# Dilated attention: the values of the class-by-class groups computed over token tiles, and brought to class order through DRAM

## The chip, the cores and the metric

The kernel runs on one core of one Trainium2 chip. The metric is the device time of one execution in microseconds (us), taken as the median over runs; lower is better. One execution with the hardware profiler on gives the trace from which the rows below are read.

The engines have short names in the rows: PE is TensorE (matrix products), PEld its loading of the stationary operand ("weights" of a product, whatever they hold), DVE is VectorE, ACT is ScalarE, POOL is GpSimd, SP is SyncE, which here issues transfers. A name with q at its end (SPq) is the queue of an engine.

## The reference, cut to what matters

The program is a network of two blocks. The first has a token mixer over 512 tokens of 1024 features; one of the mixer's two branches is dilated attention with three groups of four heads of 128 channels. Group 0 has dilation 1, group 1 dilation 4, group 2 dilation 16. A query attends to keys that are a multiple of the dilation before it, and the three groups' outputs are weighted by a softmax over their denominators:

```
proj = h @ w_in                                   # queries, keys, values of all groups, side by side
for gi, (win, dil) in enumerate(ATT_GROUPS):      # (128, 1), (512, 4), (2048, 16)
    aq, ak, av = parts[4 + 3 * gi], parts[5 + 3 * gi], parts[6 + 3 * gi]
    ...
    o, lse = dilated_group(heads(aq, ...), heads(ak, ...), heads(av, ...), tab, win, dil)
...
wts = softmax(stack(lses), axis=0)
att = einsum('gbhs,gbhsd->bshd', wts, stack(outs)).reshape(B, S, 512)
```

With 512 tokens, groups 1 and 2 attend only among tokens that are equal modulo 4. The change concerns `av` of these two groups alone: the product of the normalised input `h` (512 tokens by 1024 features) with 256 columns of `w_in` at a time.

## The kernel before, in words

`h` is kept feature-major on the chip: eight tiles `s.hh[k]` and eight `s.hl[k]` of 128 features by 512 tokens, the coarse and the fine part of each number. A panel of weights (`panel`) is loaded from DRAM in full precision (tile `wr`, two buffers, by SP) and split into a coarse part `wh` by ACT (L145) and a fine part `wl` by DVE (L134), each in two halves of four feature tiles, four buffers each, so two panels. Every product of two such numbers is three matmuls, `mm3` at L197, L198 and L199: coarse with coarse, coarse with fine, fine with coarse.

`gemm_a` gives feature-major results: the weights are the stationary operand and all 512 tokens move past them. `gemm_b` gives token-major results: 128 tokens of `h` are the stationary operand, a contiguous slice `s.hh[k][:, sl]`, and 256 columns of weights move. One token tile of 256 columns is 8 feature tiles by 3 matmuls, so 24 matmuls into one PSUM tile `mm` (three buffers).

`dilated` (L861) handles the four heads in two pairs. For each pair it first computes the values, 256 columns for each of three groups. Group 0's go through `gemm_b` into `av`. Those of groups 1 and 2 are wanted class by class: four classes of 128 tokens (token 4i + r is row i of class r). The kernel before takes them so from the product: the stationary operand is every fourth token of `h`, a view with a step of four elements:

```
classes = lambda t: t.rearrange("p (i r) -> p r i", r=4)
...
for k in range(KT):
    self.mm3(ps, classes(s.hh[k])[:, r], classes(s.hl[k])[:, r], w.hi(k), w.lo(k), k == 0, k == KT - 1)
nc.scalar.copy(v[:, r], ps)
```

That is L890; ACT copies each finished tile into `avc` (L891). A pair has 2 groups x 4 class tiles, so the program has 16 such tiles of 24 matmuls. The class values are used much later in the pair, by L978, after queries, keys, scores and the softmax: `po` is accumulated from `avc` as stationary operand and the transposed weights of the softmax `apc`. Then follow, for each of the pair's two heads, six panels of queries and keys (128 columns, 24 matmuls of 512 moving tokens each) by `gemm_a`.

Each engine runs its own instructions in a fixed order. SP's queue holds the loads of the weight panels: a load waits until its `wr` buffer has been split. The splitting of a panel's half waits until PE has read the same half of the panel two before it. POOL is used for some transfers (issued in software) and a few elementwise operations elsewhere in the program.

Of the kernel before, what the change touches and what calls it, by code (L numbers as in the profile page):

```python
# [37 lines left out]
class Stream:  # L38
    """One token stream: feature-major residual, its tokens and modulation."""
# [13 lines left out]
    def parts(self, n=2):  # L53
        """Views of the stream by tokens."""
        res = []
        for i in range(n):
            p = Stream(self.n // n, ctx=self.ctx)
            p.sl = slice(i * p.n, (i + 1) * p.n)
            p.of, p.col = self, self.col
            for nm in ("x", "hh", "hl"):  # L60
                if getattr(self, nm) is not None:
                    setattr(p, nm, [t[:, p.sl] for t in getattr(self, nm)])
            res.append(p)
        return res
# [14 lines left out]
class Net:  # L79
# [71 lines left out]
    def rsqrt(self, h, n):  # L151
        """1/sqrt(v) of a small fp32 tile, given -v/2: estimate from its bits and Newton steps."""
# [15 lines left out]
    def panel(self, src, r0, kt, c0, ncol, maps=False):  # L168
        """Columns of a weight matrix in two parts; maps: 4 heads x 2 maps x 32 columns, map by map."""
# [31 lines left out]
    def gemm_a(self, w, kt, ncol, s, evac, ks=None, ms=None):  # L201
        """Feature-major products: evac(m, stream, psum [128 features, tokens])."""
# [8 lines left out]
    def gemm_b(self, w, kt, ncol, s, evac):  # L211
        """Token-major products: evac(token tile, stream, psum [128 tokens, columns])."""
        for tt in range(s.nt):
            sl = slice(tt * P, (tt + 1) * P)
            ps = self.ps((P, ncol))
            for k in range(kt):
                self.mm3(ps, s.hh[k][:, sl], s.hl[k][:, sl], w.hi(k), w.lo(k), k == 0, k == kt - 1)
            evac(tt, s, ps)

# [1 line left out]
    def columns(self, items, tag, eng=None):  # L221
        """items: (name, DRAM rows [r, 128]); returns name -> [128, r] columns."""
# [18 lines left out]
    def squares(self, xs, acc=None, ks=range(KT), g=None):  # L241
        """Sum of squares over feature tiles (times a gain), added to acc."""
# [12 lines left out]
    def rms_cols(self, xs, n, acc=None, r=None):  # L255
        """1/rms per token (of x * r), token-major [128, n/128]."""
# [16 lines left out]
    def bcast(self, r, nt, tag="at"):  # L273
        """Token-major columns [128, nt] to every partition: [128, nt*128]."""
# [6 lines left out]
    def norm(self, s, r=None):  # L281
        """1/rms of every token, on all partitions."""
# [3 lines left out]
    def apply(self, s, acol, bcol, ks=range(KT)):  # L286
        """h = x * rstd * a + b, split in two parts."""
# [13 lines left out]
    def pair(self, s):  # L301
        """The two parts of a stream's eight feature tiles."""
# [13 lines left out]
    def ada_tasks(self, src, vec, conds):  # L316
        """Tasks for columns vec*1024.. of cond @ src + bias; conds: (silu cols, out cols, bias cols)."""
# [21 lines left out]
    def ada_first(self, src, cs, o, b):  # L339
        """The first two vectors, by halves of the features: one on TensorE, one on DVE."""  # L340
# [30 lines left out]
    def ada_finish(self, acc, o, b, vec, halves=(0, 1), when=lambda ins: ins):  # L371
        """Sum over partitions of the accumulated products, plus the bias."""
# [10 lines left out]
    def scale1(self, g, sc):  # L383
        """g * (1 + sc)"""
# [5 lines left out]
    def feed_forward(self, w1, w2, streams, between=None, first=None, last=None, late=None):  # L390
        """x += g2 * relu(h @ w1)^2 @ w2 for streams that share the weights, by groups of the hidden width.

        first: two parts for the first panels, and what to do before the last products of the former;
        last: (part of a stream, what to do after its products) for the last panel; late: what to do before it."""
# [52 lines left out]
    def project_norm(self, w_src, pairs, acols, bcols, ks=None):  # L447
        """x += g1 * (y @ w), then the modulated norm of x; what feed_forward is to do first.

        The streams (two, or two halves of one) take turns, so that one's norm hides behind the other's products."""  # L450
# [34 lines left out]
    # ==== first block ====================================================  # L485
    def first_block(self):
# [17 lines left out]
        # x to feature-major, with its mean squares on the way  # L504
# [74 lines left out]
        # gate of the retention branch  # L579
# [17 lines left out]
        # gate of the attention branch, attention output, merge  # L597
# [48 lines left out]
    def first_norm(self, xs, g):  # L646
        """The norm that closes the first block, then the input of the second."""
# [29 lines left out]
    def bias_tables(self):  # L677
        """Relative-position bias by distance as Toeplitz tables in DRAM."""
# [19 lines left out]
    def retention(self, s, w_in, v):  # L698
# [45 lines left out]
        def scores(dec, q, k):  # L744
            """Decayed scores, keys on partitions."""
# [34 lines left out]
        def outputs(hd, sc, v, between):  # L780
            """Token-major outputs, normalised over the head's channels, then feature-major."""
# [79 lines left out]
    def dilated(self, s, w_in):  # L861
        """Dilated attention, its three groups under one softmax.

        The first group keeps the tokens' order. The others attend only among tokens that are equal modulo 4,
        so theirs is class by class: 4 classes of 128 tokens, each a block of its own."""
# [11 lines left out]
        for pair in range(2):  # L877
            vv = []
            for g in range(3):
                w = self.panel(w_in, 0, KT, 6144 + g * 1536 + 1024 + pair * 256, 256)  # L880
                if g == 0:
# [3 lines left out]
                    continue  # L885
                v = self.t([P, 4, 256], "avc")
                for r in range(4):
                    ps = self.ps((P, 256))
                    for k in range(KT):
                        self.mm3(ps, classes(s.hh[k])[:, r], classes(s.hl[k])[:, r], w.hi(k), w.lo(k), k == 0, k == KT - 1)  # L890
                    nc.scalar.copy(v[:, r], ps)  # L891
                vv.append(v)
            for hp in range(2):
# [64 lines left out]
                # the first group's weights, keys on partitions: queries of block 1's keys, then of blocks 0, 2, 3  # L958
# [27 lines left out]
    def weigh(self, perm, both):  # L986
        """Factors of two softmax parts under a common one, each in its own order of the tokens.

        both[:, 0]: [128, part, 4, (maximum, sum)], the first part's tokens in order, the second's class by class.
        Each part's figures go to the other's order by a product that spreads them, between masks that pick."""  # L990
# [29 lines left out]
    # ==== second block ===================================================  # L1020
# [24 lines left out]
    def second_loads(self):  # L1045
        """Constants of the second block and the context, on their way to the chip."""
# [27 lines left out]
    def second_setup(self, ld):  # L1074
        """What the loads allow: context feature-major, bias rows, constants of the first layer."""
# [7 lines left out]
        # neighbourhood bias rows widened to 64 offsets, replicated for Toeplitz reads  # L1083
# [36 lines left out]
    def layer_consts(self, l, c):  # L1120
        nc = self.nc
        # spatial gating: weights transposed, norm vectors on every partition
# [5 lines left out]
        # differential attention: lambda and the scaled norm gain  # L1128
# [14 lines left out]
    def nbias(self, l, h):  # L1143
        """Negated neighbourhood bias of a head, [128 queries, 3 kinds of column window, 8 rows, 32 columns].

        Queries of a block are 8 rows by 16 columns, so the offsets between them and the keys step evenly
        through the replicated table."""
# [13 lines left out]
    def fourier(self, w_in, s, y):  # L1161
        """Real part of the transform over channels and tokens.

        Tokens k*nt + r of the output come from sums over blocks of 128 tokens of the input, weighted by powers
        of -1 and -i, with a transform of 128 tokens each; the weighted sums are formed before the channels'
        transform, the imaginary ones (classes 1 and 3 of four) after it."""
# [63 lines left out]
    def gelu2(self, out, ps):  # L1230
        """Twice the tanh-form gelu."""
# [8 lines left out]
    def gating(self, w_in, s, y, c, l):  # L1240
# [12 lines left out]
        # of twice the activation: a quarter of its variance, half of the gain  # L1253
# [24 lines left out]
    def heads(self, w, s, o, scale=None):  # L1278
        """Queries or keys of the differential branch, with their rotary embedding: o [4 heads x 32, map, part, tokens]."""
# [17 lines left out]
    def keys_values(self, w_in, s, fill=iter(()), ahead=False):  # L1297
        """Keys and values of both attention branches."""
# [32 lines left out]
    def windows(self, v, tag):  # L1331
        """Values by column window: [128 = 4 rows x 32 columns, window, half of the rows, 256]."""
# [33 lines left out]
    def attend_values(self, e, vs, head, po, eng=None):  # L1366
        """Transpose a [128 queries, keys] tile, then multiply by the values of a head and its neighbour."""
# [16 lines left out]
    def neighbour(self, yn, head, qb, qn, kx, kc, st, vx, vc, bt, po):  # L1384
        """Softmax attention of one head over the neighbourhood (if bt) and the context; logits come negated."""
# [37 lines left out]
    def stack(self, dst, src, head, sel):  # L1423
        """Both maps of a head as four stacked parts with tokens on the free axis, by TensorE."""
# [11 lines left out]
    def ctx_stacks(self, s, head, st):  # L1436
        """Stacked queries and keys of a context head."""
# [9 lines left out]
    def stacks(self, s, head, st=None):  # L1447
        """Stacked queries and keys of both branches for a head, moved between partitions by DMA."""
# [20 lines left out]
    def differential(self, s, yd, ssq, head, qb, qst, kst, vs, c, po):  # L1469
# [16 lines left out]
        # first map less lambda times the second, in units of the first one's denominator  # L1486
# [14 lines left out]
    def diff_norm(self, s, yd, ssq, h0, h1):  # L1501
        """Norm over the channels of each head."""
# [9 lines left out]
    def begin(self, s, l, step=KT):  # L1512
        """Modulated input of a layer's mixer, by steps of feature tiles; x spilled meanwhile."""
# [342 lines left out]
```

## Time and profile before

| what | value |
|---|---|
| runs before, median of 3 | 2887.05 us |
| lowest and highest | 2879.89 and 2893.06 us |
| the profiled execution, first to last instruction | 2886.3 us |
| PE busy in it | 2826.1 us (98%) |
| DVE, ACT, POOL busy | 1711.2, 1064.5, 103.5 us |
| mean granted TensorE clock | 0.992 of full speed |

The trace gives no time of the profiled execution apart from the span of its instructions; that span stands 0.75 us below the median of the runs. A busy share says only how long an engine was not idle; matmuls overlap each other in it, so PE can be busy all the time and still be slow. How fast it goes is read from the distance between the starts of matmuls or between finished tiles.

### The profile page before, as it was taken

Reading aid. Unit: us, or ns where it says so; the run is one execution under the profiler, and the core shown is the slowest. Engines: PE = TensorE matmul, PEld = TensorE weight load, DVE = VectorE, ACT = ScalarE, POOL = GpSimd, SP = SyncE. Lnnn points to the kernel's source line nnn. Section 1 sums busy time; section 2 is a strip of 40 time slices with the busy share of each in tenths; the row PEclk is TensorE's granted clock in tenths of the full one; section 3 lists DMA queues with packets and bytes.
Section 4 is the critical chain, followed back from the end, with each engine's and each line's share of the span. In section 5 each row is a group of like instructions: output and inputs, shape, how many; then the busy total and the mean of one; then the engine's idle time right before and its main releaser. Section 6 shows DMA issues by size and latency. Waiting matters only on the chain.

```text
span 2886.3 us, 38355 instructions
## 1 busy us (share of the span) xinstructions
PE 2826.1 (98%) x15364; PEld 2400.8 (83%) x15364; DVE 1711.2 (59%) x3154; ACT 1064.5 (37%) x1982; POOL 103.5 (4%) x143
## 2 busy tenths in 40 slices
PE   7999999999999999998999999999999999999999
PEld 4888888989888888778887788888888988888887
DVE  6667776252466888788648663443445848654434
ACT  4433432132334233245437442222223537433323
POOL 3000000000002000001000100000000000100000
PEclk9999999999999999999979999999999999999999
DMA  7455344131345555755324321112112433333231
GB/s 268 137 176 189 131 134 137 55 116 49 109 136 185 180 181 193 233 179 165 98 55 103 107 77 60 59 59 73 59 59 84 141 101 81 117 102 99 91 101 60
DMA packets 269124, 342.16 MB, mean 119 GB/s; under 512 B 18360, under 2 KB 218162, under 8 KB 268688
## 3 DMA queue, kind: packets, MB, share of 16 engines
q1 hardware_dynamic: 254880, 315.19, 34.8%
q10 hardware_dynamic: 10896, 14.72, 1.5%
q0 software_dynamic: 3168, 9.79, 1.2%
q8 instruction: 121, 1.98, 0.3%
q14 instruction: 59, 0.48, 0.1%
HBM read 313.38 MB, written 18.41 MB: 115 GB/s over the span
## 4 chain that ended last, share of the span: by engine, by line
PE 84%; DVE 8%; DMA 5%; ACT 2%; issue 1%; SPq 0%; DVEq 0%; POOL 0%; ACTq 0%
PE mm L198 24%; PE mm L197 24%; PE mm L199 24%; PE po L1380 2%; DVE wl L134 2%; DVE ada L141 2%; DMA wr<-in_ada_w 1%; PE tr L1374 1%; DMA wr<-in_w_in 1%; DMA wr<-in_w_ada 1%; PE s L1481 1%; ACT wh L145 1%; DMA wr<-in_w_ff 1%; PE tr L377 1%; PE at L197 1%
## 5 line engine op out<-in xcount | busy, mean ns | idle before, releaser
L134 DVE TENSOR_TENSOR wl<-wr,wh 128x1024 fp32r<-128x1024 f32 (+1 forms) x442 | 495.2, 1126 | 410.1 <-ACT wh L145 400.9
L145 ACT CAST wh<-wr 128x1024 fp32r<-128x1024 f32 (+1 forms) x442 | 425.7, 969 | 838.9 <-PE mm L198 674.0
L197 PE MATMUL mm<-h,wh 128*128 128x512 f32 (+1 forms) x1712 | 651.3, 382 | 3.6 <-ACT h L131 2.6
L198 PE MATMUL mm<-h,wh 128*128 128x512 f32 (+1 forms) x1712 | 654.1, 383 | 0.4 <-DVE h L141 0.4
L199 PE MATMUL mm<-h,wl 128*128 128x512 f32 (+1 forms) x1712 | 653.5, 383 | 0.5 <-DVE wl L134 0.5
L197 PEld LDWEIGHTS mm<-h,wh 128*128 128x128 f32 x1712 | 320.6, 188 | 67.9 <-ACT h L131 3.9
L198 PEld LDWEIGHTS mm<-h,wh 128*128 128x128 f32 x1712 | 321.3, 188 | 66.8 <-DVE ada L141 1.7
L199 PEld LDWEIGHTS mm<-h,wl 128*128 128x128 f32 x1712 | 321.6, 188 | 61.4 <-DVE wl L134 0.9
L198 PE MATMUL mm<-mid,wh 128*128 128x512 f32 (+1 forms) x864 | 335.0, 388 | 0.2 <-DVE mid L134 0.2
L197 PE MATMUL mm<-mid,wh 128*128 128x512 f32 (+1 forms) x864 | 334.7, 388 | 0.0
L199 PE MATMUL mm<-mid,wl 128*128 128x512 f32 (+1 forms) x864 | 334.1, 387 | 0.0
L141 DVE SCALAR_TENSOR_TENSOR ada<-wr,cs,ada 128x1024 f32<-128x1024 f32 x168 | 212.5, 1279 | 35.0 <-DMA wr<-in_ada_w 22.8
L197 PE MATMUL mm<-wh,h 128*128 128x256 f32 x704 | 212.1, 301 | 0.0
L199 PE MATMUL mm<-wh,h 128*128 128x256 f32 x704 | 211.1, 300 | 0.0
L198 PE MATMUL mm<-wl,h 128*128 128x256 f32 x704 | 210.9, 300 | 0.0
L131 ACT ACTIVATE f<-mm 128x256 f32<-128x256 f32 (+2 forms) x192 | 99.5, 520 | 263.0 <-PE mm L199 260.9
L198 PEld LDWEIGHTS mm<-mid,wh 128*128 128x128 f32 x864 | 162.2, 188 | 36.7 <-DVE mid L134 1.3
L199 PEld LDWEIGHTS mm<-mid,wl 128*128 128x128 f32 x864 | 162.2, 188 | 36.3
L197 PEld LDWEIGHTS mm<-mid,wh 128*128 128x128 f32 x864 | 162.2, 188 | 35.6
L141 DVE SCALAR_TENSOR_TENSOR x<-mm,modx,x 128x512 f32<-128x512 f32 (+1 forms) x116 | 84.8, 731 | 175.6 <-PE mm L199 174.1
L134 DVE TENSOR_TENSOR f<-f 128x512 f32<-128x512 f32 (+2 forms) x172 | 99.4, 585 | 143.6 <-ACT f L131 142.5
L198 PEld LDWEIGHTS mm<-wl,h 128*128 128x128 f32 x704 | 150.9, 214 | 0.8 <-issue 0.2
(451 smaller groups left out, 4309.5 us busy)
## 6 DMA issues: line engine op xcount, KB each, us to landing
wr<-in_w_ff SPq DMA_DIRECT2D x96, 1024.0 KB
wr<-in_w_in SPq DMA_DIRECT2D x69, 1024.0 KB
wr<-in_ada_w SPq DMA_DIRECT2D x48, 1024.0 KB
wr<-in_w_ada SPq DMA_DIRECT2D x16, 1024.0 KB
wr<-in_w_in SPq DMA_DIRECT2D x24, 512.0 KB
awr<-in_w_ada SPq DMA_DIRECT2D x16, 512.0 KB
wr<-in_w_ret_out SPq DMA_DIRECT2D x8, 1024.0 KB
wr<-in_w_out SPq DMA_DIRECT2D x8, 1024.0 KB
```

Of the source, the lines that this page charges most:

```text
L131: return self.nc.scalar.activation(out=out, in_=in_, func=func, **kw)
L134: return self.nc.vector.tensor_tensor(out=out, in0=a, in1=b, op=op)
L141: return self.nc.vector.scalar_tensor_tensor(out=out, in0=a, scalar=s, in1=b, op0=op0, op1=op1)
L145: self.nc.scalar.copy(hi, src)
L197: mm(out, lhsT=ah, rhs=bh, start=start, stop=False)
L198: mm(out, lhsT=ah, rhs=bl, start=False, stop=False)
L199: mm(out, lhsT=al, rhs=bh, start=False, stop=stop)
L377: when(self.nc.tensor.transpose(ps[:, j], acc[:, m * P:(m + 1) * P], self.ident))
L1374: self.nc.tensor.transpose(tp[:, i], e[:, (b0 + i) * P:(b0 + i + 1) * P], self.ident)
L1380: self.nc.tensor.matmul(po, lhsT=pt[:, kb], rhs=vs[kb][:, head // 2 * P:(head // 2 + 1) * P], start=kb == 0, stop=kb == nk - 1)
L1481: nc.tensor.matmul(ps[:, k0:k1], lhsT=qst[:, mp, qs], rhs=kst[:, mp, k0:k1], start=True, stop=True)
```

## The change

The 16 class tiles become 16 token tiles: `gemm_b` computes the values of groups 1 and 2 as it does those of group 0. ACT copies each token tile from PSUM into half of a scratch tile `f` (pool of five). After each second tile POOL issues a transfer of 256 KB from it to a DRAM tile `vcls` of 512 tokens by 256 columns. After the fourth, POOL issues one transfer of 512 KB from `vcls` to `avc`, in which partition i takes rows 4i to 4i + 3, a contiguous piece of 4 KB; so `avc` holds token 4i + r at partition i, class r, as before. L978 then reads the same `avc`. All comments and docstrings of the file are also taken out, which moves line numbers by 8 behind this place and nothing else.

```
@@ -883,12 +883,20 @@
                     vl = self.r([P, 4, 256], "av")
                     self.gemm_b(w, KT, 256, s, lambda tt, s_, ps: self.split(ps, vh[:, tt], vl[:, tt]))
                     continue
+
+                d = self.tc.dram_tile([512, 256], F32, name="vcls")
+                halves = []
+
+                def evac(tt, s_, ps):
+                    if tt % 2 == 0:
+                        halves.append(self.t([P, 2, 256], "f"))
+                    nc.scalar.copy(halves[-1][:, tt % 2], ps)
+                    if tt % 2:
+                        nc.gpsimd.dma_start(out=d[(tt - 1) * P:(tt + 1) * P].rearrange("(t p) f -> p t f", p=P),
+                                            in_=halves[-1])
+                self.gemm_b(w, KT, 256, s, evac)
                 v = self.t([P, 4, 256], "avc")
-                for r in range(4):
-                    ps = self.ps((P, 256))
-                    for k in range(KT):
-                        self.mm3(ps, classes(s.hh[k])[:, r], classes(s.hl[k])[:, r], w.hi(k), w.lo(k), k == 0, k == KT - 1)
-                    nc.scalar.copy(v[:, r], ps)
+                nc.gpsimd.dma_start(out=v, in_=d.rearrange("(i r) f -> i r f", r=4))
                 vv.append(v)
             for hp in range(2):
```

In the order of instructions, PE, DVE and SP have the same rows before and after (the matmuls keep their shapes; only which columns of `h` they load differs). On ACT, in the stretch of a pair's class values, these rows stood before (a number behind x counts equal rows in a run):

```order
L145 CAST wh<-wr 128x1024
L891 COPY avc<-mm 128x256 x3
L145 CAST wh<-wr 128x512
L891 COPY avc<-mm 128x256
L145 CAST wh<-wr 128x512
```

And these stand there now:

```order
L145 CAST wh<-wr 128x1024
L893 COPY f<-mm 128x256 x3
L145 CAST wh<-wr 128x512
L893 COPY f<-mm 128x256
L145 CAST wh<-wr 128x512
```

Only the copy's destination differs; the splitting of the next panels keeps its place behind the third and the fourth copy. On POOL, before, nothing stood between the setup of the dilated attention (`perm`, `apt`) and the loads for the second block (`xt`, `blk`):

```order
L868 DMA perm_4576<-in_k_perm 128x384
L876 MEMSET apt_4578 128x128 x3
L876 MEMSET apt_4579 128x128 x3
L1054 DMA xt_7782<-in_ctx_2 128x1024
L1054 DMA xt_7783<-in_ctx_2 128x1024
L1056 DMA blk_7786<-in_k_blk 128x2
```

Now twelve transfers stand between them, three for each of four groups of values; these are the first two groups' (the first pair's):

```order
L876 MEMSET apt_4578 128x128 x3
L876 MEMSET apt_4579 128x128 x3
L895 DMA vcls_4754<-f_4780 128x2x256
L895 DMA vcls_4754<-f_4834 128x2x256
L899 DMA avc_4863<-vcls_4754 128x1024
L895 DMA vcls_4875<-f_4901 128x2x256
L895 DMA vcls_4875<-f_4955 128x2x256
L899 DMA avc_4984<-vcls_4875 128x1024
L895 DMA vcls_5880<-f_5906 128x2x256
```

Each L899 waits until both writes of its `vcls` have landed, and the rows behind it on POOL wait with it.

## Rows read from the trace of the kernel before

**Rows 1.** The page: span, busy time of the engines, and the chain's shares by engine.
```profile
span 2886.3 us, 38355 instructions
PE 2826.1 (98%) x15364; PEld 2400.8 (83%) x15364; DVE 1711.2 (59%) x3154; ACT 1064.5 (37%) x1982; POOL 103.5 (4%) x143
PE 84%; DVE 8%; DMA 5%; ACT 2%; issue 1%; SPq 0%; DVEq 0%; POOL 0%; ACTq 0%
```

**Rows 2.** Three stretches: group 0's token tiles, then class tiles of either pair.
```profile
core 0: us, PE busy (x) PEld busy (x) DVE busy (x) ACT busy (x) POOL busy (x), PEclk, DMA share, GB/s
505.10:516.00 10.90, 10.90 (x97) 10.90 (x96) 5.45 (x9) 3.72 (x6) 0.00 (x0) 1.00 0.48 146
518.00:562.60 44.60, 44.60 (x197) 44.60 (x198) 5.73 (x14) 4.37 (x10) 0.00 (x0) 1.00 0.09 24
664.00:708.80 44.80, 44.80 (x192) 44.80 (x192) 4.45 (x6) 5.50 (x12) 0.00 (x0) 1.00 0.09 24
```

**Rows 3.** ACT in order of time, first pair: start, duration, line, operation, idle before.
```profile
508.04 0.37 ACT L145 CAST av<-mm 128x256 fp32r<-128x256 f32 x1 [1.38 <-PE mm L199]
...
516.20 0.37 ACT L145 CAST av<-mm 128x256 fp32r<-128x256 f32 x1 [0.31 <-PE mm L199]
...
523.57 0.37 ACT L891 COPY avc<-mm 128x256 f32<-128x256 f32 x1 [6.05 <-PE mm L199]
...
562.76 0.37 ACT L891 COPY avc<-mm 128x256 f32<-128x256 f32 x1 [2.18 <-PE mm L199]
...
565.28 0.62 ACT L145 CAST wh<-wr 128x512 fp32r<-128x512 f32 x1 [1.63 <-PE mm L198]
...
570.78 0.62 ACT L145 CAST wh<-wr 128x512 fp32r<-128x512 f32 x1 [1.62 <-PE mm L198]
```

**Rows 4.** ACT in order of time, first and last class copy of the second pair.
```profile
669.46 0.37 ACT L891 COPY avc<-mm 128x256 f32<-128x256 f32 x1 [4.33 <-PE mm L199]
...
709.04 0.37 ACT L891 COPY avc<-mm 128x256 f32<-128x256 f32 x1 [2.21 <-PE mm L199]
```

**Rows 5.** Weight loads of one line: token tiles (505.2 to 516), class tiles (523.6 to 562.6).
```profile
L198 PEld LDWEIGHTS mm<-wl,h 128*128 128x128 f32 x32 | 6.0, 188 | 0.0
...
L198 PEld LDWEIGHTS mm<-wl,h 128*128 128x128 f32 x56 | 18.5, 330 | 0.0
```

**Rows 6.** PE's waits, 500 to 850 us: total, times, longest (first and last of five).
```profile
PE tr L964 <- DVE apt L134: 1.2, 1, 1.2
...
PE tr L964 <- DVE sr L138: 0.2, 1, 0.2
```

**Rows 7.** SP's queue: issue of three weight panels of 512 KB (start, duration).
```profile
519.91 0.37 SPq L165 DMA_DIRECT2D wr<-in_w_in  x1
...
542.01 0.37 SPq L165 DMA_DIRECT2D wr<-in_w_in  x1
...
564.41 0.37 SPq L165 DMA_DIRECT2D wr<-in_w_in  x1
```

**Rows 8.** A panel of 1 MB on the chain of waits; the rate of transfers in one us.
```profile
638.75 5.02 DMA wr<-in_w_in
...
644.00:645.00 1.00, 1.00 (x12) 1.00 (x11) 0.81 (x7) 1.00 (x2) 0.00 (x0) 1.00 1.10 349
```

**Rows 9.** First reads of the class values, either pair: ns min/median/max, first and last start.
```profile
L978 PE MATMUL po<-apc,avc x16: 275/275/377, 616.6 to 618.4; 128*128 128x128 f32 x16
...
L978 PE MATMUL po<-apc,avc x32: 275/275/377, 762.6 to 809.7; 128*128 128x128 f32 x32
```

**Rows 10.** POOL: two kinds of its transfers (us to landing), its longest issue, two neighbours in time.
```profile
ebuf<-erow POOLq DMA_DIRECT2D x16, 240.0 KB, 7.3
xt<-in_ctx POOLq DMA_DIRECT2D x2, 512.0 KB, 3.8
...
L1107 POOL DMA_DIRECT2D acc<-in_sgu_w x2 | 1.6, 808 | 61.7 <-PE tr L262 61.7
...
858.37 0.54 POOL L1054 DMA_DIRECT2D xt<-in_ctx  x1 [438.25 <-DVE f L134]
```

## The prediction

> **What bounds the kernel now.** I read the page first. PE is busy for 98% of the span and holds 84% of the chain that ended last [rows 1]: time taken from PE's own stream comes off the end, unless PE then has to wait for something. A busy share does not say how fast PE goes, so the next view was that of busy time by stretches, over the place of the change. PE is busy all through, with the granted clock at 1.00, both where it makes group 0's token tiles and where it makes the class tiles [rows 2]. But it does 97 matmuls in 10.9 us in the first stretch and 197 in 44.6 us in the second. Same engine, same clock, same shape of matmul, half the rate.
>
> The distance between finished tiles gives the exact price, since every tile of either kind is 24 matmuls. ACT takes a token tile out of PSUM at 508.04 us and the third one after it at 516.20 [rows 3]: 8.16 / 3 = 2.72 us a tile, 113 ns a matmul. It takes the first class tile at 523.57 and the seventh after it at 562.76 [rows 3]: 39.19 / 7 = 5.599 us a tile, 233 ns a matmul. In the second pair the same seven steps run from 669.46 to 709.04 [rows 4]: 39.58 / 7 = 5.654 us.
>
> What differs between the two kinds is only the stationary operand: contiguous columns of `h` in the one, every fourth column in the other. The rows of the weight loads show it there: the same instruction takes 188 ns in token tiles and 330 ns in class tiles [rows 5]. The durations of one instruction overlap and are partly modelled, so I use them for where the time sits and not for how much; the amount is from the tile steps.
>
> Last I read PE's waits from 500 to 850 us, which hold the whole dilated attention. There are five, from 1.2 us down to 0.2 us, 2.8 us in all, and each is for DVE or ACT in the softmax; none is for a weight panel [rows 6]. So here PE sets the pace and the panels keep up.
>
> **What goes away.** 8 class tiles at 5.599 and 8 at 5.654 become 16 token tiles at 2.72 us: 8 x 2.879 + 8 x 2.934 = 23.0 + 23.5 = 46.5 us. The lower bound of a tile after is that of group 0's row, the same shapes from the same `h`; I know no reason for it to be faster. If the second pair kept its 1% more (5.654 to 5.599), its tiles would take 2.75 us and the sum would lose 0.2 us.
>
> **What is added on ACT and PE: nothing.** ACT's copies keep number, place and size, 0.37 us each [rows 3], with another destination. PE has the same 384 matmuls. A PSUM tile must be emptied in time: three buffers, a tile every 2.72 us, and between two copies at most one split of 0.62 us for a later panel [rows 3]. Group 0 lives with the same arrangement at this rate today, and PE shows no wait there.
>
> **What is added on POOL and in DRAM.** Twelve transfers: eight writes of 256 KB, four reads of 512 KB. POOL is idle around them: its next instruction before the change starts at 858.37 us after 438 us of idle time [rows 10], so neither their issues (at most 0.81 us each, the longest that POOL shows [rows 10]) nor the wait of each read for its two writes delays other work of POOL. Queued behind a waiting read are the next group's writes; they hold `f` tiles, but a pair uses four of the five, and the second pair comes some 100 us after the first.
>
> The bounce is new to this trace in this place, so I bound it from both sides. POOL's transfers land in 3.8 us (512 KB from DRAM) to 7.3 us (240 KB within DRAM) [rows 10]. The last write and the read, one behind the other, then take 2 x (0.5 + 3.8) = 8.6 to 2 x (0.8 + 7.3) = 16.2 us; I take the longer. The cover is long: the last class copy of the first pair ends at 563.13 us [rows 3] and PE's first product that needs `avc` starts at 616.6 [rows 9], 53.5 us later; in the second pair it is 709.41 [rows 4] to 762.6 [rows 9], 53.2 us. Both ends move by the same amount, so 37 us are left over. Cost: nothing. Without that cover it would be 16.2 us for each pair.
>
> **What comes closer: the weight panels.** A panel's load is issued once the `wr` tile two before it is split, and panels now follow each other faster. The loads to look at are those for the queries and keys behind the class tiles. One is issued at 519.91, before the class tiles begin to tell; the next at 542.01, after the first class group [rows 7], and ACT splits it at 565.28 [rows 3], 23.3 us later. One whole class group lies between; it shrinks from 22.4 to 10.9 us, so 11.8 us are left. The third is issued at 564.41 [rows 7] and split at 570.78 [rows 3]; both are behind the class tiles, so its 6.4 us stay. A panel of 1 MB, twice the size, landed in 5.02 us [rows 8], so both loads land in time if they have the queue alone.
>
> Now they share the transfer engines with the bounce. At the rate that the trace shows under full load, 349 GB/s [rows 8], the last write and the read of a group, 786 KB together, take 2.25 us. Behind them a panel would land in at most 5.02 + 2.25 = 7.3 us: 0.9 us over the third load's 6.4. If that falls together in both pairs it costs 1.8 us. A panel of half the size should need some 1.5 us less, and the read starts only after its writes have landed, by which time the panel mostly has too. I take 0, and keep 1.8 as the bound.
>
> **Sum.** 2886.3 - 46.5 = 2839.8 us for an execution like the profiled one. Its span is 0.75 us below the median of the runs, so the median after should be 2840.5; I say 2840.
>
> **Rivals.** First: *the gain is partly given back to late panels.* If a panel waits behind the whole landing of the read (7.3 + 0.5 us) and not just for its share of the bandwidth, it is late by 5.02 + 7.8 - 6.4 = 6.4 us, about 13 us over both pairs: 2853 us. For it: both use the same 16 transfer engines. Against: DMA is busy for 9% in the class stretches [rows 2], and the two kinds are in different queues.
>
> Second: *no change.* If the slower rate did not come from the step of four, the token tiles would run at 233 ns a matmul and the time would stay at 2886 us. Against it: in the rows nothing else differs between the two stretches [rows 2, 5]. A rule of the Trainium skill ("TensorE: Matmul & The Clock Gate", section "LDWEIGHTS (loading the stationary operand)") gives a weight load as columns / 1.2 in ns, 107 ns for 128, and makes it depend on the number of columns alone. By that rule both kinds of tile would cost the same and this edit would save nothing. The trace differs: 188 and 330 ns for the same 128 columns.
>
> Third, *slower:* the read of the bounce lands after PE wants `avc`. The place is L978, with the softmax and the output of the head queued behind it. It would begin to cost when the bounce takes more than 53 us, and eat the whole gain at 53 + 23 = 76 us for each pair, 4.7 times the longest estimate; at 90 us the time would be 2886.3 + 2 x 14 = 2914 us. What could stretch it so far is POOL being kept from issuing. The Trainium skill ("SBUF — State Buffer", section "A bandwidth-pool intuition that's wrong (but worth ruling out)") says that an issue of POOL can be blocked by DVE, 620 ns growing to 3100 ns beside a copy. Against the rival: DVE is busy for 5.7 of the 44.6 us of the class stretch [rows 2], and POOL's longest issue in the whole trace is 0.81 us [rows 10]. Even 3.1 us for each of three issues of a group stays inside the cover.
>
> **How the numbers follow.** The forecast, 2840 us, gets 0.90; late panels, 2853, 0.05; no change, 2886, 0.03; slower, 2914, 0.02. The three runs before lie from 2879.89 to 2893.06, 7 below and 6 above the median, and two medians of such runs are compared. Around 2840 I therefore take 8 us downwards, and upwards 9, which also takes in the 1.8 us of the panels, the 0.2 us of the second pair and two thirds of the way to the first rival: 2832 to 2849. What lies outside is the other rivals and some scatter, less than 2 in 10. A measurement of this kernel can tell about 0.5% (14 us) from no change. The forecast and the first rival are both beyond that, so faster 0.95, same 0.03, slower 0.02.
>
> **What would show it.** In the profile after: steps of 2.7 us between the copies into `f`; the weight loads of these tiles at 188 ns; a stretch of about 21.8 us for the two groups of a pair where there were 44.8; no wait of PE for `wl` or `wh` in the queries and keys behind it; `avc` landed some 40 us before L978, which shows no wait for a transfer. Wrong would be: steps that stay above 5 us (second rival), waits of PE for panels of more than 2 us (first), a wait of L978 for DMA (third), or a time that comes back elsewhere, in the panels of the second block, which nothing in this trace would explain.

## The result, and the profile after

Four runs of the changed kernel have a median of 2839.48 us (2835.82 to 2845.01); four of the kernel before (the three of the table further up and one more) 2883.47 us (2879.49 to 2893.06). The ratio is 0.9845, with a 95% interval from 0.9822 to 0.9868: 1.5% faster, 44 us between the medians. The profiled execution after has a span of 2841.0 us, 45.3 us less than the one before [rows 1]. The page's first rows after, span and busy time:

```profile
span 2841.0 us, 38392 instructions
PE 2786.3 (98%) x15364; PEld 2361.2 (83%) x15364; DVE 1710.5 (60%) x3154; ACT 1065.3 (37%) x1982; POOL 111.5 (4%) x155
```

PE is busy for 98% as before, for 40 us less. The same stretches as in [rows 2], after (the second and third line hold most of the two groups of the first and of the second pair; they do not start and end exactly with a tile, so the amount is again read from the copies below):

```profile
core 0: us, PE busy (x) PEld busy (x) DVE busy (x) ACT busy (x) POOL busy (x), PEclk, DMA share, GB/s
505.10:516.00 10.90, 10.84 (x97) 10.64 (x96) 5.56 (x10) 3.50 (x6) 0.00 (x0) 1.00 0.48 146
518.00:539.60 21.60, 21.60 (x183) 21.23 (x182) 3.93 (x10) 5.27 (x12) 3.46 (x5) 1.00 0.34 112
641.00:662.00 21.00, 21.00 (x181) 21.00 (x180) 3.11 (x4) 4.38 (x10) 2.70 (x4) 1.00 0.36 113
```

What filled some 45 us now takes less than half, at the same granted clock. ACT's copies give the step from tile to tile, to be set beside [rows 3] and [rows 4] (last token tile of group 0, then first and last of the changed tiles, first pair and second):

```profile
513.77 0.37 ACT L145 CAST av<-mm 128x256 fp32r<-128x256 f32 x1 [0.31 <-PE mm L199]
...
518.57 0.37 ACT L893 COPY f<-mm 128x256 f32<-128x256 f32 x1 [3.48 <-PE mm L199]
...
537.61 0.37 ACT L893 COPY f<-mm 128x256 f32<-128x256 f32 x1 [0.74 <-PE mm L199]
...
639.53 0.37 ACT L145 CAST av<-mm 128x256 fp32r<-128x256 f32 x1 [0.32 <-PE mm L199]
...
642.35 0.37 ACT L893 COPY f<-mm 128x256 f32<-128x256 f32 x1 [1.51 <-PE mm L199]
...
662.14 0.37 ACT L893 COPY f<-mm 128x256 f32<-128x256 f32 x1 [0.79 <-PE mm L199]
```

First pair: 19.04 / 7 = 2.72 us a tile. Second pair: 19.79 / 7 = 2.83 us, 4% more than forecast. From group 0's last copy to the pair's last one it took 46.56 us before and takes 23.84 now in the first pair [rows 3]: 22.7 saved. In the second pair it took 45.23 (to 709.04 [rows 4], from group 0's last copy in the kernel before, the row below) and takes 22.61: 22.6 saved. Together 45.3 us, as much as the difference of the spans.

```profile
663.81 0.37 ACT L145 CAST av<-mm 128x256 fp32r<-128x256 f32 x1 [0.26 <-PE mm L199]
```

That what lies outside the two stretches cancels out is chance, and the two profiles are one execution each: the one after is 2.4 us ahead where the first stretch begins, and loses 0.9 us between the two and 1.6 us behind them. Its granted clock was 0.66 from 630 to 635 us, between the pairs, where the one before kept 1.00 (650 to 660 us). The weight loads of the changed tiles, as in [rows 5]:

```profile
L198 PEld LDWEIGHTS mm<-wl,h 128*128 128x128 f32 x57 | 10.7, 188 | 0.0
```

188 ns, as for group 0, where the class tiles had 330. The bounce on POOL, behind the first pair's second group (last write and read, start and duration of the issue; then the first products that read `avc`, and, from the same view of the tile, how long the pair's two reads from DRAM took to land):

```profile
538.27 0.72 POOL L895 DMA_DIRECT2D vcls<-f  x1 [4.73 <-ACT f L893]
541.50 0.55 POOL L899 DMA_DIRECT2D avc<-vcls  x1 [2.51 <-issue]
```

```profile
L986 PE MATMUL po<-apc,avc x16: 275/275/377, 591.4 to 593.2; 128*128 128x128 f32 x16
...
DMA to landing us min/median/max: 4.2/4.4/4.6
```

The values are in `avc` at about 546 us and PE wants them at 591.4. PE's waits over the whole dilated attention, as in [rows 6]:

```profile
PE tr L972 <- DVE apt L134: 1.2, 1, 1.2
PE po L198 <- DVE apt L134: 0.5, 1, 0.5
PE tr L972 <- DVE sr L138: 0.2, 1, 0.2
```

Three of the five waits of before, all within the softmax, and none for a weight panel or a transfer.

### The profile page after: what moved, and what is told of

It reads as the page before. It is cut to its first block, busy times and chain, and to the rows that moved or that the text cites. A ratio compares the mean times of both kernels' runs of the same rounds, so it can differ in the third digit from the quotient of the medians.

```text
span 2841.0 us, 38392 instructions
## 1 busy us (share of the span) xinstructions
PE 2786.3 (98%) x15364; PEld 2361.2 (83%) x15364; DVE 1710.5 (60%) x3154; ACT 1065.3 (37%) x1982; POOL 111.5 (4%) x155
## 4 chain that ended last, share of the span: by engine, by line
PE 85%; DVE 7%; DMA 3%; issue 2%; ACT 2%; POOL 1%; SPq 0%; DVEq 0%; ACTq 0%; POOLq 0%
PE mm L198 25%; PE mm L197 25%; PE mm L199 24%; PE po L1388 3%; DVE wl L134 2%; PE tr L1382 1%; DVE ada L141 1%; DMA wr<-in_ada_w 1%; PE s L1489 1%; PE tr L377 1%; ACT wh L145 1%; DMA wr<-in_w_ff 1%; PE at L197 1%; PE at L198 1%; PE at L199 1%
## 5 line engine op out<-in xcount | busy, mean ns | idle before, releaser
L141 DVE SCALAR_TENSOR_TENSOR ada<-wr,cs,ada 128x1024 f32<-128x1024 f32 x168 | 212.5, 1280 | 32.9 <-DMA wr<-in_ada_w 22.4
L197 PE MATMUL mm<-wh,h 128*128 128x256 f32 x704 | 196.7, 279 | 0.0
L199 PE MATMUL mm<-wh,h 128*128 128x256 f32 x704 | 195.9, 278 | 0.0
L198 PE MATMUL mm<-wl,h 128*128 128x256 f32 x704 | 195.8, 278 | 0.0
L198 PEld LDWEIGHTS mm<-wl,h 128*128 128x128 f32 x704 | 132.5, 188 | 0.8 <-issue 0.2
```

Of the source, the lines that this page charges most:

```text
L141: return self.nc.vector.scalar_tensor_tensor(out=out, in0=a, scalar=s, in1=b, op0=op0, op1=op1)
L197: mm(out, lhsT=ah, rhs=bh, start=start, stop=False)
L198: mm(out, lhsT=ah, rhs=bl, start=False, stop=False)
L199: mm(out, lhsT=al, rhs=bh, start=False, stop=stop)
```

## The experiments

The theory to test: the whole gain is the time that PE loses by loading a stationary operand with a step of four; the bounce through DRAM (a group's two writes and the read behind them) is free because it is hidden. The rivals: the bounce costs or delays something after all; the rate of the class tiles has another cause; the cover (the time from a pair's last copy to PE's first product that reads `avc`) is smaller than counted. The four kernels of runs 1 to 4 ran on one chip, the four of 5 to 7 on a second, and the three of 8 to 10 on a third; each was timed against the kernel before on its own chip.

**1. The bounce without the faster products.** The class products stay, and each two of them go through DRAM:

```
for r in range(4):
    ...                                   # class product with step four, as before
    if r % 2 == 0:
        half = self.t([P, 2, 256], "f")
    nc.scalar.copy(half[:, r % 2], ps)
    if r % 2:
        nc.gpsimd.dma_start(out=rows4[:, r - 1:r + 1], in_=half)
v = self.t([P, 4, 256], "avc")
nc.gpsimd.dma_start(out=v, in_=rows4)
```

> The class products of before with the step of four, and the twelve transfers of the change added: each pair of class tiles goes through a scratch tile to DRAM and comes back to avc in the same class order, so the outputs stay the reference's. My theory (the gain is the weight loads' step, the transfers are hidden): the time of before, 2883 to 2887 us, class tiles at 5.60 and 5.65 us, no wait of PE for a weight panel and none of L978's products for a transfer. Rival (the transfers delay weight panels): up to 13 us above before, with PE waits for wh or wl in the queries and keys behind the class tiles.

Measured: 2888.49 us against 2885.61, ratio 1.0007 (0.9994 to 1.0019). Twelve transfers more change nothing that can be measured; the interval leaves at most 5.5 us. Tiles step by 5.60 and 5.65 us as before. The rival of late panels gets nothing here; in this kernel, though, panels follow each other at the old distance, so this run alone does not speak for the changed kernel.

**2. The faster products without the bounce.** It leaves out the order of classes:

```
v = self.t([P, 4, 256], "avc")
self.gemm_b(w, KT, 256, s, lambda tt, s_, ps: nc.scalar.copy(v[:, tt], ps))
```

> The token tiles of the change, copied by ACT straight into avc in the tokens' order; no scratch tile, no transfer. It leaves out the bringing to class order, so the values of groups 1 and 2 meet the wrong weights. My theory: the time of the changed kernel within 0.2% (2836 to 2845 us). Rival (the bounce costs something hidden in the 2839.5): 2 to 13 us faster than the changed kernel. It also tells whether the 2.83 us of a token tile in the second pair, where the first pair and group 0 have 2.72, comes from the transfers: if so it is 2.72 here in both pairs, if not it is 2.83 again.

Measured: 2841.38 us, ratio 0.9845 (0.9824 to 0.9867), the same as the changed kernel's. So the products alone give the gain, and the bounce takes nothing from it that these runs could tell (either interval is some 6 us to each side). The tiles had 2.72 us in both pairs in this profile. That the transfers make the 2.83 us of the changed kernel's second pair does not follow: run 3 has transfers and 2.72 us in its second pair, and run 9, without any, starts the matmuls of group 0's last token tile in its second pair 117 to 118 ns apart (23 steps from 637.76 to 640.46 us), which is the slow rate.

**3. Half of the change.** Group 1 through token tiles and DRAM, group 2 as before (`if g == 2:` ahead of the old loop).

> The change for group 1 alone; group 2 keeps the class products, so the outputs stay the reference's. My theory (a price per tile): half the gain, 22 to 24 us, so 2860 to 2864 us, token tiles of 2.7 to 2.8 us and class tiles of 5.6 us side by side in a pair. Rival (the gain hangs on something that the pair has once, such as when the weight panels come): clearly more or less than half.

Measured: 2867.21 us, 3 us above the forecast range. The ratio, 0.9919 (0.9894 to 0.9944), is a gain of 23 us (16 to 31), the distance of the medians 18 us; both are compatible with half of the whole, and neither is sharp. The profile is. ACT's copies show both kinds of tile side by side (the first pair's last copy of group 0, then first and last of either kind; then the second pair's last copy of group 0 and its last class copy):

```profile
514.66 0.37 ACT L145 CAST av<-mm 128x256 fp32r<-128x256 f32 x1 [0.31 <-PE mm L199]
519.50 0.37 ACT L902 COPY f<-mm 128x256 f32<-128x256 f32 x1 [3.52 <-PE mm L199]
...
527.99 0.37 ACT L902 COPY f<-mm 128x256 f32<-128x256 f32 x1 [0.80 <-PE mm L199]
533.64 0.37 ACT L893 COPY avc<-mm 128x256 f32<-128x256 f32 x1 [4.76 <-PE mm L199]
...
550.60 0.37 ACT L893 COPY avc<-mm 128x256 f32<-128x256 f32 x1 [2.21 <-PE mm L199]
...
651.81 0.37 ACT L145 CAST av<-mm 128x256 fp32r<-128x256 f32 x1 [0.26 <-PE mm L199]
...
685.30 0.37 ACT L893 COPY avc<-mm 128x256 f32<-128x256 f32 x1 [2.21 <-PE mm L199]
```

From group 0's last copy to the pair's last one it takes 35.94 and 33.49 us here, against 46.56 and 45.23 before: 10.6 and 11.7 saved, 22.4 together, half of the 45.3. In the first pair there are three steps of 2.83 us, then four (from 527.99 on) of 5.65. The slow variant of the token tile is here in the first pair; the second pair of the same profile, with the same transfers, has 2.72 for the token tiles.

**4 to 6. Other steps.** The kernel before with another view of `h` as stationary operand, everything else as it was (the views alone, in place of `classes(t)[:, r]`):

```
step2 = t.rearrange("p (i r) -> p r i", r=2)[:, r % 2, r // 2 * P:(r // 2 + 1) * P]
step3 = t[:, :384].rearrange("p (i r) -> p r i", r=3)[:, r % 3]
step8 = full.rearrange("p a (i r) -> p r (a i)", r=8)[:, r + 4 * (k % 2), k // 2 * P:(k // 2 + 1) * P]
```

> The kernel before with a step of two in place of four: each tile takes every second token of half the sequence. It leaves out the right class order, so the values of groups 1 and 2 are of other tokens. If any step costs as much as a step of four: 2883 to 2887 us. If the load's time grows evenly with the step (113 ns a matmul at one, 233 at four): 153 ns, tiles of 3.7 us, 16 x 0.95 us above the changed kernel, 2855 us. If a step is free as long as two neighbouring elements share 16 bytes, as the Trainium skill's SBUF page has it (SBUF - State Buffer, section Door 1: The DMA port swizzle): tiles of 2.72 us and 2839 us. I hold the last for likeliest, since a matmul of 256 columns hides a load of up to 113 ns.

> The stationary operand takes every third token of the first 384 (the fourth tile repeats the first); values of groups 1 and 2 are therefore of other tokens. The step of two cost 2.88 us a tile, next to 2.72 at step one. If the price is one of memory lines of 16 bytes (the Trainium skill's rule), a step of 12 bytes touches a new line with three elements of four: some 4.9 us a tile. If it grows evenly with the step from two (2.88) to four (5.60): 4.2 us.

> The stationary operand takes every eighth token, over two neighbouring feature tiles at once; the products of groups 1 and 2 are therefore of mixed features and not the reference's. If the price is that of a new line of 16 bytes for every element, four is the end of it: 5.6 us a tile and the time of before, 2883 to 2890 us. If it grows with the step: 11 us a tile and 2970 us.

Times: 2845.47 us at a step of two (ratio 0.985, 0.983 to 0.9871), 2860.19 at three and 2890.68 at eight (one run each, beside 2891.01 of the kernel before). The time at two is 6 us above the 2839 that I held for likeliest, within the scatter of its four runs (2837.81 to 2847.33); the tiles account for 2.6 us of it. The steps of the tiles tell more. First and last copy of the first pair at two, at three and at eight:

```profile
519.29 0.38 ACT L892 COPY avc<-mm 128x256 f32<-128x256 f32 x1 [3.58 <-PE mm L199]
...
539.45 0.37 ACT L892 COPY avc<-mm 128x256 f32<-128x256 f32 x1 [0.81 <-PE mm L199]
```

```profile
520.25 0.37 ACT L892 COPY avc<-mm 128x256 f32<-128x256 f32 x1 [4.62 <-PE mm L199]
...
549.52 0.37 ACT L892 COPY avc<-mm 128x256 f32<-128x256 f32 x1 [1.46 <-PE mm L199]
```

```profile
521.76 0.37 ACT L893 COPY avc<-mm 128x256 f32<-128x256 f32 x1 [6.24 <-PE mm L199]
...
562.33 0.37 ACT L893 COPY avc<-mm 128x256 f32<-128x256 f32 x1 [2.27 <-PE mm L199]
```

A seventh of each difference, and a 24th of that for one matmul:

| step, elements of 4 bytes | us a tile | ns a matmul | pieces of 16 bytes touched by 128 columns |
|---|---|---|---|
| 1 | 2.72 | 113 | 32 |
| 2 | 2.88 | 120 | 64 |
| 3 | 4.18 | 174 | 96 |
| 4 | 5.60 | 233 | 128 |
| 8 | 5.80 | 241 | 128 |

The price is that of the step, and it stops growing at four: two to four nearly doubles it, four to eight adds 3%. It follows the last column: 174 / 96 and 233 / 128 are both 1.8 ns, and 64 x 1.8 = 116 ns stands next to the 113 that a matmul of 256 columns takes anyway. A step of two is cheap but not free, 120 ns for 113, and neither these 7 ns nor the 3% at eight come out of the count. The Trainium skill ("SBUF — State Buffer", section "Door 1: The DMA port swizzle") says that the memory is read in lines of 16 bytes and that an access that goes to a new line pays; the last column is worked out from that line size, and the rows agree with it. That the price stops at 16 bytes is measured; that lines of memory are the reason is argued, since all operands here have elements of 4 bytes and no other alignment was run. My figure of 4.9 us for a step of three was wrong: three new lines for four elements are three quarters of 5.60, 4.2 us, which is also what even growth from two to four gives, so that run did not tell those two apart. The run at eight did.

**7. A longer chain in the bounce, twice.** More copies from DRAM to DRAM, each behind the one before, between the writes and the read:

```
for _ in range(2):                        # 6, 10 in the others
    d2 = self.tc.dram_tile([512, 256], F32, name="vhop")
    nc.gpsimd.dma_start(out=d2, in_=d)
    d = d2
```

> The changed kernel with two more copies from DRAM to DRAM (512 KB each, issued by POOL, each behind the one before) between the writes and the read of a bounce; outputs stay the reference's. Four more copies a pair, some 8 us each (7.3 to landing and 0.5 to issue, from the copies between DRAM tiles in rows 10): 32 us more, and the bounce of the changed kernel lands 45 us before L986 wants it. My theory (the bounce is hidden with that much to spare): no change from 2839.5 us, within 0.2%. Rival (its traffic or its waits cost): slower by 5 us or more.

> The same with six more copies in each bounce, twelve a pair, some 94 us of them. My theory: the cover of 45 us is used up, and PE waits at the first L986 of either pair for what is left: 45 to 50 us a pair if a copy takes 8 us, 2930 to 2940 us; in general 12 copies less 45 us. Rival (the order of the waits gives more room than I counted, or the copies of the two groups overlap): less than half of that.

Two hops: 2840.58 us, ratio 0.9828 (0.9804 to 0.9852): nothing lost. Six hops: 2847.32 us, ratio 0.9856 (0.9834 to 0.9878), 6.7 us above two hops on the same chip. My figure of 45 to 50 us a pair was wrong, but the cover was not: a copy was issued some 5 us after the one before and not 8, and the second group's first copies went out among the first group's. In the first pair the last read was issued at 587.28 us, lands within 4.0 to 5.6 us, and PE asked at 593.6 without a wait. In the second pair it came some 3 us late. The issue of that last read, PE's first product behind its landing, and the wait:

```profile
717.00 0.57 POOL L903 DMA_DIRECT2D avc<-vhop  x1 [4.65 <-DMA vhop<-vhop]
...
721.63 3.35 PE L990 MATMUL po<-apc,avc 128*128 128x128 f32 x14 [2.69 <-DMA avc<-vhop]
...
PE po L990 <- DMA avc<-vhop: 2.7, 1, 2.7
```

The stretches around it, with six hops and then with two, where PE did not wait (granted clock in the last column but two):

```profile
720.00:725.00 5.00, 3.37 (x16) 0.59 0.08 33
725.00:730.00 5.00, 5.00 (x22) 0.73 0.00 2
...
720.00:725.00 5.00, 5.00 (x25) 1.00 0.01 2
725.00:730.00 5.00, 5.00 (x24) 1.00 0.51 171
```

The wait is 2.7 us; with it and behind it the granted clock is 0.59 and 0.73 in two stretches of 5 us, where with two hops it is 1.00. Read us by us it is 0.50 from 721 to 727 us, the lower of the two levels (1.2 GHz in place of 2.4), and PE resumed at 721.63; about 6 us at half the clock are an estimated 3 us lost. The first pair's tiles also ran at 2.83 us here and at 2.72 with two hops, 0.9 us. Together that is 6.6 us, and the two profiled spans differ by 6.4 (2848.5 and 2842.1).

**8. The chain made too long.**

> As six_hops with ten copies in each bounce. There a copy took 4.8 us to landing and a little over 5 us with its issue, and the chain ended when PE wanted the values: no wait in the first pair, 2.7 us in the second. Eight more copies a pair, some at the same time as the other group's, should make PE wait 30 to 40 us at the first L986 of either pair: 2905 to 2925 us. If the wait stays under 10 us a pair, the cover is not what set six_hops' limit.

Measured: 2907.64 us in one run, within the range.

```profile
PE po L990 <- DMA avc<-vhop: 65.9, 2, 33.5
```

One wait in each pair, 32.4 and 33.5 us, behind the first two products of L990. So the place where a late bounce costs is the one named in the prediction. The waits also measure the cover. From the end of a pair's last copy to the end of PE's wait it took 87.4 us (539.40 to 626.84) and 86.0 us (699.43 to 785.47) here, and 56.4 us (665.26 to 721.63) in the second pair of six hops; less the waits that leaves 53.7 to 53.9 us, where 53.2 and 53.5 were counted from [rows 3], [rows 4] and [rows 9].

**9. No bounce at all, with class tiles.** The panels of groups 1 and 2 lie side by side (two halves of the features, 512 columns each), so that one load with a step of four serves both groups:

```
self.mm3(ps, classes(s.hh[k])[:, r], classes(s.hl[k])[:, r], w.hi(k % 4), w.lo(k % 4), ...)   # 512 columns
...
for i in range(2):
    nc.scalar.copy(vs[i][:, r], ps[:, i * 256:(i + 1) * 256])
```

> The class tiles with the step of four, but one load of the stationary operand serves both groups: the panels of groups 1 and 2 lie side by side, so a matmul moves 512 columns where it moved 256, and half the matmuls are left; no transfer through DRAM, outputs stay the reference's. My theory (a load of 128 columns at step four takes 233 ns and hides behind whatever moves meanwhile): a matmul every 233 to 236 ns, 5.6 to 5.66 us for the two groups' class together, 22.5 us a pair where the changed kernel has 21.8 to 22.6: 2839 to 2843 us. Rival (a strided load holds up the moving operand also): load and columns add up, 350 ns or more a matmul, 34 us a pair, 2862 us.

Measured: 2842.03 us, ratio 0.9855 (0.984 to 0.9869), within the scatter of the changed kernel. ACT's copies, two at a time, of the first pair's first and last class:

```profile
521.51 0.65 ACT L897 COPY avc<-mm 128x256 f32<-128x256 f32 x2 [6.49 <-PE mm L199]
...
538.66 0.65 ACT L897 COPY avc<-mm 128x256 f32<-128x256 f32 x2 [0.81 <-PE mm L199]
```

17.15 / 3 = 5.72 us for a class of both groups, 238 ns a matmul. With 256 columns the same load let a matmul pass every 233 ns, so 256 columns more cost 5 ns; 512 moving columns past a contiguous operand take 229 ns in the queries and keys. So load and columns do not add up: the longer of the two sets the pace, within a few ns.

**10. The bounce from ACT's queue.** `nc.scalar` for `nc.gpsimd` in the three transfers.

> The changed kernel with its twelve transfers issued by ACT and not by POOL. Each read then waits in ACT's queue for its writes (2.8 us to landing), ahead of a copy out of PSUM or of the splitting of a weight panel. From the trace of the changed kernel: behind a pair's last class tile the split of the next panel comes about 1.3 us later than its 540.1 us, and PE wants that panel only at 548. My theory: no change, within 0.3% of 2839.5 us. Rival (ACT's waits reach PE): PE waits for wh or for a PSUM tile, 1 to 3 us a pair, 2842 to 2846 us.

Measured: 2843.43 us, ratio 0.985 (0.9832 to 0.9868). PE has no wait longer than those of the softmax in it. The median is 4 us above the changed kernel's, with runs from 2835.96 to 2845.7, and it lies in the forecast range as well as in the rival's, so a cost of a few us is neither shown nor excluded.

## Why the prediction was right

**Where PE loses time.** The prediction read the loss from the step of finished tiles and put it down to the stationary operand's step. The runs with the products alone (2) and with half of them (3) show that the gain is in the products and goes by the tile. Those with other steps (4 to 6) show that it is the step of the view, since nothing else was changed there.

**The size.** Forecast 46.5 us for the profiled execution, 45.3 came; between the medians it is 44.0. The missing 1.2 us lie in two terms. Token tiles of the second pair took 2.83 us and not 2.72, 0.9 us over eight tiles; the prediction allowed 2.75. And the first pair saved 22.7 us and not 23.0. The 0.75 us that the sum adds from the span to the runs mix that distance with scatter: the run profiled after took 2842.74 us for its span of 2841.0, 1.74 more. The forecast of 2840 us stands 0.5 us from the measured median of 2839.48, and that it is so close is luck: the sum began at one execution of 2886.3 us, the median before fell by 3.6 us with one run more, and the four runs after lie 9 us apart.

**ACT and POOL at nothing.** No copy makes PE wait. POOL's issues take 0.55 to 0.74 us here (the 0.81 us of [rows 10] is the mean of two, 0.79 and 0.83; nothing hangs on it); a write landed in 2.8 us (median of eight) and a read in 4.2 to 4.6, so the last write and the read took about 8 us, a little under the estimate of 8.6 to 16.2.

**The cover.** 53.5 us were counted between the last copy and the first use; after the change it is 537.61 + 0.37 to 591.4, 53.4 us. The runs with more copies use it up: no wait when the data comes within it, waits at L986's place when not, and 53.7 to 53.9 us by the length of those waits.

**The panels.** The second of the three loads in [rows 7] is now issued at 528.37 us and split at 540.12, 11.75 us later, for which 11.8 was worked out; the third at 539.25 and 545.62, 6.4 us as before. SP's rows and ACT's of the changed kernel:

```profile
528.37 0.37 SPq L165 DMA_DIRECT2D wr<-in_w_in  x1
...
539.25 0.37 SPq L165 DMA_DIRECT2D wr<-in_w_in  x1
```

```profile
540.12 0.62 ACT L145 CAST wh<-wr 128x512 fp32r<-128x512 f32 x1 [1.62 <-PE mm L198]
...
545.62 0.62 ACT L145 CAST wh<-wr 128x512 fp32r<-128x512 f32 x1 [1.63 <-PE mm L198]
```

Both splits were held up by PE and not by the load (the releaser in brackets). The bounce's share of the transfer engines cost nothing; the bound of 1.8 us was not needed, and the first rival fell.

**The rivals.** No change: refuted by the runs with other steps, and with it, for this kind of operand, the rule of the Trainium skill ("TensorE: Matmul & The Clock Gate", section "LDWEIGHTS (loading the stationary operand)") that a load depends on the number of its columns alone: 128 columns allowed a matmul every 113 to 241 ns, by their step. Slower through a late read: the mechanism exists at the place named and takes effect when the bounce is long enough. With ten extra copies of each group (8) the whole gain is lost and more, 2907.64 us where the kernel before has 2883.66 on that chip. The prediction's reckoning holds for it: from a pair's last copy to PE's going on it took 86.0 and 87.4 us, on average 10.7 beyond the 76 at which the gain is used up, and 2886.3 + 2 x 10.7 is 2908 us. What was weighed there as a cause, POOL kept from issuing by DVE, shows in none of the twelve issues (at most 0.74 us).

## What to carry to other kernels

In this kernel a stationary operand of 128 columns with 4-byte elements is best taken with a step of one or two. At three, four or eight elements its load takes longer than 256 moving columns, and PE looks fully busy all the same; compare the distance between finished tiles of the same shape at different places to see it. When a strided order is needed, there are two ways out that cost nothing here: compute in the natural order and let transfers bring the result to the other order, if it is needed long enough after; or let more columns move past each strided load. How long is long enough can be read before the change, from the last producer to the first consumer, and it held to within 1 us when it was used up on purpose.

## What was not expected of the hardware

Token tiles have two rates at the same granted clock. In most stretches a tile takes 2.72 us; in some it takes 2.83 (118 ns a matmul for 113), and then all tiles of the stretch do. The changed kernel had the slow rate in the second pair, as had two and ten hops and the bounce from ACT's queue; six hops had it in both pairs, the kernel of run 3 in the first and not in the second, that of run 2 in neither. Class tiles also have two rates, 5.60 and 5.65 us [rows 3, 4], but not together with those of the token tiles: the second pair of run 3 has 2.72 and 5.65 side by side. It is not the granted clock, which is 1.00 in these stretches, and matmuls of 512 columns behind the slow stretch in the second pair start every 229 ns as elsewhere. What sets it stays open; it is worth 0.9 us for a pair's eight tiles.

A short wait of PE can cost more than its length: in run 7, 2.7 us of waiting were followed by the clock's lower level, some 3 us more. Behind the long waits of run 8 the clock was low as well (0.78 on average from 626 to 640 us), but there the surcharge does not show in the total: 65.9 us of waiting, and a span 64.8 us above the changed kernel's (2905.8 for 2841.0), one execution each.
